# Searching the 256th largest indexer score: bit by bit, or by halving a guessed interval

## The chip, the core and the metric

The kernel runs on one core of a Trainium2 chip. The metric is the device time of one execution in microseconds, from the core's first instruction to its last. The engines named below are PE (TensorE), DVE (VectorE), ACT (ScalarE), POOL (GpSimd) and SP (SyncE, which here only issues transfers). Each engine takes its instructions in order, and an instruction that waits for another engine holds up all that stand behind it in its own queue.

## The reference, cut to what matters

A decoder block on 1024 tokens of width 1024: an indexed sparse attention and a latent attention side by side, merged by sigmoid gates, then a gated MLP. The part that the change touches is the choice of 256 keys for each query:

```python
iscore = jnp.einsum('bqh,bqhs->bqs', wib, jax.nn.relu(dots))
iscore = jnp.where(causal, iscore, -jnp.inf)
_, idx = lax.top_k(iscore, topk)          # topk = 256
ksel = k[bidx, idx]
...
sc = jnp.where(valid[:, :, None, None, :], sc, -jnp.inf)
p = jax.nn.softmax(sc, axis=-1)
```

Ties go to the lower column. The gates are `jax.nn.sigmoid(g_a)` and `jax.nn.sigmoid(g_b)`, with `g_a` and `g_b` two products of the normalised input with 1024 columns of `w_in` each.

## The kernel before, in words

Tokens are cut into 8 blocks of 128 queries. A program tests first whether the positions rise; if so the causal path runs, in which block b sees 128(b+1) keys, else a general path (`emit`, branch at L1808; the end of both is one drain at L1867). Blocks 0 and 1 have no more than 256 keys; for blocks 2 to 7 the kernel must find, in each of the 128 rows, the 256th largest of 384 to 1024 float32 scores.

`topk` does that for blocks 2, 3, 4 in one call and 5, 6, 7 in another. It takes the score as a 32-bit integer that is ordered as the score is: sixteen rounds settle its upper half, sixteen its lower half. A round counts in each block how many are below a candidate, on DVE by one instruction with an accumulator (L779), and for blocks 2 and 7 on ACT as a sum of signs (L776). Three small instructions on DVE then make the next candidate for three blocks at once (L787, L788, L789, 128x3 each). L760, L761, L802 and L804 make the integer halves. A tail of seven instructions for each block (L826 to L833) counts again in float32, ranks the ties with a scan (L829), and makes an additive mask of 0 or a large number, which SP writes to DRAM (L837) for the attention that comes later.

Three other streams of work are interleaved with the search.

- **Indexer.** PE makes the scores head by head (L702), ACT takes them from PSUM (L721), DVE adds them up (L726).
- **Gates.** 16 weight tiles of `w_g`, each a [128, 1024] piece in float32, used as a high and a low part. ACT makes the high part (L148), POOL the low part (L154). A tile gives two halves of 512 columns. A half is 24 products on PE (L178, L179, L180) into one of four PSUM banks; DVE takes it out and multiplies it with the norm's factor (L875); ACT applies the sigmoid (L877) and issues the write to DRAM (L878). In this text the halves are called #0 to #31. Eight small products (L557) stand ahead of #16.
- **Latents.** After #19 PE does 24 transposes (L896) in two groups of 12, into the same four PSUM banks. ACT and DVE take them out (L904, L905). Their inputs are eight loads by SP (L894) into six buffers: those of blocks 6 and 7 go where blocks 0 and 1 were. #20 to #27 follow, then the preparation of the latent attention.

The order on each engine is settled when the program is built, by priorities and due times of a scheduler; it is not written out in the source. The four banks mean that PE can finish a half only three halves (3 x 5.44 us) ahead of the one that DVE takes out. The high part of tile t stands in ACT's queue behind the sigmoid of half #(2t-4), so PE's first product of tile t (half #2t) also comes behind DVE's L875 of that half.

Of the kernel before, what the change touches and what calls it, by code (L numbers as in the profile page):

```python
# [50 lines left out]
LEAD = 1.0, 1.0  # L51
QDUP = 1
# [33 lines left out]
def chunks(W):  # L86
    """Column pieces of a row of W scores: (start, length), each in a PSUM bank of its own."""
    if W <= 512:
        return [(0, W)]
    return [(0, W // 2), (W // 2, W // 2)]  # L90


def weave(*lists, lead=1.0):
    """Call the closures of several lists, each list in its order, evenly mixed (the first list ahead, if lead < 1)."""
    items = [((k + 0.5) / len(x) * (1.0 if n else lead), n, f) for n, x in enumerate(lists) for k, f in enumerate(x)]
    for _, _, f in sorted(items, key=lambda t: t[:2]):
        f()


def skewed(first, second, lag):  # L100
    """The closures of two lists in turn, the second list some places behind."""
    out = []
    for k in range(len(first) + lag):
        out += first[k:k + 1] + (second[k - lag:k - lag + 1] if k >= lag else [])
    return out


class Block:
    def __init__(self, tc, a, out, causal, consts):
# [46 lines left out]
    def rsqrt(self, pool, y, x, n):  # L156
        """y = x ** -0.5 for [P, n] float32 tiles, x > 0."""
# [7 lines left out]
        for _ in range(3):  # L165
            # y = y * (1.5 - 0.5 * x * y * y)
# [8 lines left out]
    def mm3(self, ps, lhs, rhs, start, stop, **kw):  # L175
        """ps += lhs.T @ rhs, with both given as (hi, lo)."""
# [12 lines left out]
    def rope(self, x, c, s2, tmp):  # L189
        """x [P, H, 2, n] in place; c [P, H, n], s2 [P, H, 2, n] = (-sin, sin)."""  # L190
# [13 lines left out]
    def posmask(self, pool, b):  # L204
        """[P, S] bf16: 0 where pos[k] <= pos[q], BIG elsewhere, q in block b."""
# [10 lines left out]
    def view(self, off, shape, of=None):  # L216
        """A part of a region of float32r (r0, if no other), as an array of its own."""
# [16 lines left out]
    def run(self):  # L234
# [41 lines left out]
        if self.causal:  # L276
# [3 lines left out]
            self.topk(ta, [2, 3, 4], (2,))  # L280
# [17 lines left out]
        if self.causal:  # L298
            self.topk(tk, [5, 6, 7], (7,))
# [3 lines left out]
        # r1: v of the latent attention, the output of the indexed attention, half of w_out, then the operands of the  # L303
        # MLP's weights
# [17 lines left out]
        # the first scores; the last gates leave as they are, and take their sigmoid where they are used  # L322
# [35 lines left out]
        # tx: the other half of w_out, then three sums of the normalised rows  # L358
# [34 lines left out]
    def prologue(self):  # L393
# [18 lines left out]
        # cos and sin of pos * INV, [P, NB, 16]  # L412
# [32 lines left out]
        if self.causal:  # L445
            # 0 on and below the diagonal, BIG (tri) or FILL (trif) above it
# [8 lines left out]
            v.tensor_scalar(self.trif, jp, 0.0, FILL, op0=OP.is_gt, op1=OP.mult)  # L455
        self.posi = posi
# [17 lines left out]
    def stage(self, src):  # L474
        """A [P, n <= 1024] float32 array on its way from DRAM."""
# [4 lines left out]
    def ahead(self, name, *js):  # L480
        """Start the loads of weight pieces that wload will take later."""
# [20 lines left out]
    def wload(self, pool, name, j, wb, eng_hi="act", eng_lo="pool", tags=("wh", "wl")):  # L502
        """A [P, n <= 1024] piece of a weight as (hi, lo)."""
# [48 lines left out]
    def row_scales(self, halves):  # L552
        """R: the norm's factor of every token, on all partitions."""
# [11 lines left out]
    def cproj(self, w, ncols, blocks, pss=None):  # L565
        """Projections of token blocks; the row tiles in the outer loop, as they arrive."""
# [10 lines left out]
    def chunk_kv(self, rawx, w):  # L577
# [9 lines left out]
        # the raw projections; the norm's factor r goes into the factors of the three segments  # L587
# [23 lines left out]
        rt = self.t(c, [P, NB, 2, 16])  # L611
# [15 lines left out]
    def qstack(self, raw, scale, off):  # L627
        """[P, 8 * 2 * HD], every head twice -> [P, 8 * P] float32r, per head (hi; lo) of its transpose."""
# [9 lines left out]
    def twice(self, pool, x, nh, tag, bufs=2):  # L638
        """[P, nh * HD] -> [P, nh * 2 * HD], every head twice."""
# [12 lines left out]
    def chunk_iq(self, rp):  # L652
        """The indexer's queries and scores; the projections of the indexed attention's queries between."""
# [6 lines left out]
        def query(b, ps):  # L660
            # normalised, rotated
# [29 lines left out]
    def scores(self, lhs, rhs, W, diag=False):  # L691
        """psum [P, 2, 512] (or one bank used) of sum lhs[i].T @ rhs[i] over W columns; returns its view."""
# [15 lines left out]
    def indexer(self, q, b, marks):  # L708
        """Closures: the scores of a block of queries, head after head."""
# [28 lines left out]

    def topk(self, tk, blocks, on_act=()):
        """mask_d[b] = 0 for the TOPK largest of isc[b] (ties: the lower column first), BIG elsewhere.  # L740

        The TOPK-th largest value, bit by bit: first the upper halves of the values (as ordered 16 bit
        integers), then the lower halves among the values that share the upper half found. The columns of
        the blocks in on_act are counted by ACT, as a sum of signs; a candidate lies half way between two integers."""
# [26 lines left out]
        def below(src):  # L771
            """cnt: how many of src lie below c (or, by ACT, that less how many lie above)."""
# [9 lines left out]
        def search(src, first):  # L782
            """c: the largest integer that not more than thr lie below, of 16 bits from first on."""
# [8 lines left out]
        # keys: the lower half, in the order of the values, where the upper half is that found; 0 elsewhere  # L792
# [13 lines left out]
        # the whole value  # L806
# [10 lines left out]
        for j, b in enumerate(blocks):  # L817
# [7 lines left out]
            # le = score <= t; TOPK - #(score > t) = TOPK - W + #le  # L825
# [13 lines left out]
    def chunk_a(self, rp, name):  # L839
        """Closures: q (w_c3) or k and v (w_c4) of the indexed attention, normalised and rotated, to DRAM."""  # L840
# [44 lines left out]
    def latents(self, bx):  # L885
# [11 lines left out]
                # the shared rope part of k, four times over the partitions  # L897
# [41 lines left out]
            # v: [tok, head, hi | lo], odd heads lo | hi  # L939
# [38 lines left out]
    def project(self, pr):  # L978
        """Closures: the nope parts of q and k of the heads 2 * pr and 2 * pr + 1, into [P, 512] tiles."""
# [21 lines left out]
    def operands(self, st, pr, par):  # L1001
        """Closures: fill hq and hk of one parity out of the projected tiles."""
# [18 lines left out]
    def probs(self, pool, ps, W, mask, l, tag, bufs, wide=S):  # L1021
        """Softmax rows out of ps, the negated scaled scores; mask (bf16) adds BIG where a key is out."""
# [848 lines left out]
```

## Time and profile before

| | us |
|---|---|
| median of 3 runs (1672.86 to 1680.73) | 1673.42 |
| the profiled execution: its time is its span | 1673.4 |
| PE busy, whole span | 1533.1 (92%) |
| DVE busy, whole span | 1282.6 (77%) |
| POOL busy | 909.0 (54%) |
| ACT busy | 840.6 (50%) |
| DVE busy, 260 to 358 us | 97.19 of 98.00 |
| PE busy, 260 to 358 us | 76.11 of 98.00 |
| `topk`'s counts on DVE (L779) | 122.9, in 132 instructions |

The shares of the whole span say that PE bounds the kernel. The windows say that it does not do so everywhere: there is a stretch of some 150 us in which another engine is at 96 to 99% and PE is not. A table by stretch is therefore read before any table of the whole.

### The profile page before, as it was taken

The numbers are of one execution on the slowest core, as the hardware profiler recorded it, in microseconds if no ns is written. First come the engines' busy times: TensorE is split into PE (matmuls) and PEld (weight loads), VectorE is DVE, ScalarE is ACT, GpSimd is POOL, SyncE is SP. The second block draws the span as 40 slices with busy tenths as digits, with TensorE's granted clock in tenths as the row PEclk, the third lists the DMA queues.
The fourth block names the chain that finished last, engine by engine and source line by source line (L and its number), as shares of the span: only waits on it lengthen the run. The fifth ranks groups of instructions, "written<-read, shape, count | busy, mean of one in ns | idle before, by whom it ended". The sixth has DMA issues, their size and how long they took to land. (4 is left out here: it accounts for less than half of the span.)

```text
span 1673.4 us, 21977 instructions
## 1 busy us (share of the span) xinstructions
PE 1533.1 (92%) x7310; PEld 1254.1 (75%) x7310; DVE 1282.6 (77%) x2221; ACT 840.6 (50%) x1569; POOL 909.0 (54%) x748
## 2 busy tenths in 40 slices
PE   8889998758989999999999978999999999979995
PEld 7768886547767777898878776888888887858874
DVE  7368999998567887888461887677777775896996
ACT  3545645452437778877431454444444444434444
POOL 3241121221166677765560469877777773486683
PEclk9989998888999998999999989999999999999997
DMA  7331121231120003221664113222222213964333
GB/s 231 116 104 45 48 81 67 78 117 69 55 66 13 17 25 88 90 69 51 192 206 163 57 39 100 76 76 89 91 86 76 76 51 109 348 204 139 120 113 134
DMA packets 74844, 166.25 MB, mean 99 GB/s; under 512 B 9634, under 2 KB 14114, under 8 KB 74722
## 3 DMA queue, kind: packets, MB, share of 16 engines
q1 hardware_dynamic: 64496, 142.74, 26.4%
q10 hardware_dynamic: 7634, 13.64, 2.1%
q0 software_dynamic: 2592, 8.39, 1.3%
q8 instruction: 59, 0.97, 0.3%
q14 instruction: 63, 0.52, 0.1%
HBM read 123.94 MB, written 40.53 MB: 98 GB/s over the span
## 5 line engine op out<-in xcount | busy, mean ns | idle before, releaser
L178 PE MATMUL tc<-tc,tc 128*128 128x512 f32 (+2 forms) x1420 | 548.3, 390 | 25.1 <-ACT tc L148 14.6
L180 PE MATMUL tc<-tc,tc 128*128 128x512 f32 (+2 forms) x1420 | 549.5, 388 | 14.3 <-POOL tc L154 12.6
L179 PE MATMUL tc<-tc,tc 128*128 128x512 f32 (+2 forms) x1420 | 549.7, 387 | 0.5 <-POOL tc L154 0.4
L154 POOL TENSOR_TENSOR tc<-tc,tc 128x512 fp32r<-128x512 f32 (+2 forms) x182 | 293.4, 1619 | 295.4 <-ACT tc L148 271.5
L148 ACT ACTIVATE tc<-tc 128x512 fp32r<-128x512 f32 (+1 forms) x362 | 229.1, 658 | 339.2 <-PE tc L179 222.7
L178 PEld LDWEIGHTS tc<-tc,tc 128*128 128x128 f32 x1420 | 271.9, 192 | 85.2 <-ACT tc L148 16.6
L180 PEld LDWEIGHTS tc<-tc,tc 128*128 128x128 f32 x1420 | 271.0, 191 | 74.3 <-POOL tc L154 15.9
L179 PEld LDWEIGHTS tc<-tc,tc 128*128 128x128 f32 x1420 | 271.4, 191 | 55.7 <-POOL tc L154 0.9
L154 DVE TENSOR_TENSOR tc<-tc,tc 128x512 fp32r<-128x512 f32 x184 | 216.9, 1212 | 50.8 <-ACT tc L148 44.3
L179 PE MATMUL tc<-tc 128*128 128x512 f32 x332 | 132.6, 400 | 8.7 <-DVE tc L154 8.7
L1042 POOL TENSOR_SCALAR tc<-tc,tc 128x128 f32<-128x128 f32 (+7 forms) x128 | 95.2, 748 | 68.7 <-DVE tc L1041 56.1
L180 PE MATMUL tc<-tc 128*128 128x512 f32 x332 | 132.0, 399 | 0.4 <-DVE tc L154 0.4
L178 PE MATMUL tc<-tc 128*128 128x512 f32 x332 | 125.8, 401 | 7.1 <-ACT tc L148 7.0
L779 DVE TENSOR_SCALAR_CACHE_REDUCE tc<-tc,tc 128x512 bf16<-128x512 int16 (+7 forms) x132 | 122.9, 940 | 0.6
L1040 ACT ACTIVATE tc<-tc,tc 128x128 f32<-128x128 f32 (+7 forms) x128 | 96.3, 753 | 34.0 <-DVE tc L1034 14.5
L1574 DVE SCALAR_TENSOR_TENSOR tc<-tc,tc,tc 128x1023 f32<-128x1023 f32 x44 | 64.3, 1464 | 53.7 <-ACT tc L1573 53.6
L702 PE MATMUL tc<-tc 128*128 128x384 f32 (+4 forms) x352 | 92.1, 376 | 13.1 <-DVE tc L635 6.6
L776 ACT ACTIVATE tc<-tc,tc 128x384 bf16<-128x384 uint16 (+2 forms) x66 | 57.9, 877 | 79.1 <-DVE tc L789 57.2
L1575 DVE SCALAR_TENSOR_TENSOR tc<-tc,tc,tc 128x1022 f32<-128x1022 f32 x44 | 94.3, 2143 | 1.4
L702 PE MATMUL tc<-tc,tc 128*128 128x512 f32 (+4 forms) x288 | 78.8, 390 | 8.6 <-ACT tc L1040 8.2
L179 PEld LDWEIGHTS tc<-tc 128*128 128x128 f32 x332 | 63.7, 192 | 24.6 <-DVE tc L154 11.8
L178 PEld LDWEIGHTS tc<-tc 128*128 128x128 f32 x332 | 63.9, 193 | 22.1 <-ACT tc L148 8.5
(257 smaller groups left out, 2579.4 us busy)
## 6 DMA issues: line engine op xcount, KB each, us to landing
tc<-tc SPq DMA_DIRECT2D x144, 256.0 KB, 3.6
tc<-in_w_up SPq DMA_DIRECT2D x44, 512.0 KB, 4.0
tc<-in_w_down SPq DMA_DIRECT2D x77, 256.0 KB, 4.1
tc<-tc ACTq DMA_DIRECT2D x52, 256.0 KB, 2.0
tc<-tc SPq DMA_DIRECT2D x20, 512.0 KB, 2.6
tc<-in_w_g SPq DMA_DIRECT2D x16, 512.0 KB, 3.7
tc<-tc POOLq DMA_DIRECT2D x24, 256.0 KB, 2.6
tc<-in_w_c SPq DMA_DIRECT2D x10, 512.0 KB, 4.2
```

The costliest lines, as they stand in the source:

```text
L148: self.last_split = nc.scalar.activation(hi, src, AF.Copy)
L154: e.tensor_tensor(lo, src, hi.bitcast(F32), op=OP.subtract)
L178: x = [mm(ps, lhs[0], rhs[0], start=start, stop=False, **kw), mm(ps, lhs[0], rhs[1], start=False, stop=False, **kw), mm(ps, lhs[1], rhs[0] ...
L179: mm(ps, lhs[0], rhs[1], start=False, stop=False, **kw),
L180: mm(ps, lhs[1], rhs[0], start=False, stop=stop, **kw)]
L702: self.last_score = mm(ps[:, j * 512:j * 512 + n], l, r[:, o:o + n], start=i == 0, stop=i == len(lhs) - 1)
L776: nc.scalar.activation(junk2[:, :W], src[b], AF.Sign, bias=c[:, j:j + 1], scale=-1.0, accum_out=cnt[:, j:j + 1])
L779: v.tensor_scalar(junk[:, :W], src[b], c[:, j:j + 1], 0.0, op0=OP.is_lt, op1=OP.add, accum_out=cnt[:, j:j + 1])
L1040: self.last_exp = nc.scalar.activation(p3, src, AF.Exp, bias=nm, scale=-1.0, accum_out=l)
L1042: nc.gpsimd.tensor_scalar(p, p, l, 0.0, op0=OP.mult, op1=OP.add)
L1574: v.scalar_tensor_tensor(o[:, 1:], x[:, :S - 1], cw[:, t, 1:2], o[:, 1:], op0=OP.mult, op1=OP.add)
L1575: v.scalar_tensor_tensor(o[:, 2:], x[:, :S - 2], cw[:, t, 0:1], o[:, 2:], op0=OP.mult, op1=OP.add)
```

## The change

In `run`, both calls of `topk` on the causal path become calls of a new function `guess`, and a call of `unsure` follows the second. `guess` takes mean and standard deviation of a part of each row's scores (`bn_stats`, L768), guesses from them an interval that holds the 256th largest score, and halves it ten times. Each round is one float32 count for each block on DVE (L786) and three small instructions (L792 to L794); ACT counts nothing. A last count at the bound follows; the scores at or above the bound are pushed down (L800), the eight largest of what is left are taken (L801), and the one that the count points to is the threshold. The tail with ties, scan and mask (L815 to L824) is as before, with one small instruction more (L820) that notes rows where the result can't be the 256th. `unsure` adds these notes up on PE (L836) and sets a flag. `emit` reads the flag after the causal path (L1913), and runs the general path, with `topk` as before, where it is set. All other lines of the diff take comments out, or put one small buffer into another place, and set nine constants on POOL.

```diff
-            self.topk(ta, [2, 3, 4], (2,))
+            self.guess(ta, [2, 3, 4])
...
-            self.topk(tk, [5, 6, 7], (7,))
+            self.guess(tk, [5, 6, 7])
+            self.unsure()
...
+HALVINGS = 10
+SPAN = {2: (-1.5, 2.2), 3: (-0.3, 1.2), 4: (0.1, 1.1), 5: (0.3, 1.1), 6: (0.4, 1.1), 7: (0.5, 1.1)}
...
+    def guess(self, tk, blocks):
...
+        for j, b in enumerate(blocks):
+            m = b * P
+            k = 1 if m <= 512 else 2
+            for i in range(k):
+                v.bn_stats(stat[j][:, i], self.isc[b][:, i * m // k:(i + 1) * m // k])
+            v.bn_aggr(mv[:, j], stat[j][:, :k])
...
+        def above(j, b):
+            W = self.width(b)
+            x = self.t(tk, [P, wide], BF16, tag="junk", bufs=1)[:, :W]
+            v.tensor_scalar(x, self.isc[b], c[:, j:j + 1], 0.0, op0=OP.is_ge, op1=OP.add, accum_out=cnt[:, j:j + 1])
+            return x
+
+        for k in range(HALVINGS):
+            for j, b in enumerate(blocks):
+                above(j, b)
+            v.scalar_tensor_tensor(cp, h, -(2.0 ** -(k + 1)), c, op0=OP.mult, op1=OP.add)
+            v.scalar_tensor_tensor(m, cnt, TOPK - 0.5, h, op0=OP.is_ge, op1=OP.mult)
+            v.scalar_tensor_tensor(c, m, 2.0 ** -k, cp, op0=OP.mult, op1=OP.add)
+        v.scalar_tensor_tensor(c, h, 1.01 * 2.0 ** -HALVINGS, c, op0=OP.mult, op1=OP.add)
...
+        for j, b in enumerate(blocks):
+            x = above(j, b)
+            rest = self.t(tk, [P, wide], F32, tag="rest", bufs=1)[:, :self.width(b)]
+            v.scalar_tensor_tensor(rest, x, -3.0e38, self.isc[b], op0=OP.mult, op1=OP.add)
+            v.max(out=best[:, j], in_=rest)
+        v.tensor_scalar(m, cnt, -1.0, float(TOPK), op0=OP.mult, op1=OP.add)
...
+            v.tensor_scalar(bad[:, js], ct[:, W - 1:W], need[:, js], None, op0=OP.is_lt)
...
+        v.scalar_tensor_tensor(bad, need, 0.5, bad, op0=OP.is_lt, op1=OP.add)
...
-    with tc.If(rising > 0) as cmp:
-        Block(tc, a, out, True, {}).run()
-    with cmp.Else():
-        Block(tc, a, out, False, {}).run()
+    with tc.If(rising > 0):
+        Block(tc, a, out, True, {"redo": redo}).run()
+    again = nc.values_load(redo[0:1, 0:1], min_val=0, max_val=1)
+    with tc.If(again > 0):
+        Block(tc, a, out, False, {}).run()
```

In the program after the change lines have other numbers: L148 becomes L150, L477 L486, L726 L735, L837 L825, L875 L975, L877 L977, L878 L978, L894 L994, L896 L996, L905 L1005.

ACT's queue between the sigmoids of two successive halves in the gates, before:

```order
L877 ACTIVATE tc_1971<-tc_1971 128x512
L776 ACTIVATE tc_3158,tc_3153<-tc_3141,tc_3154 128x1024
L776 ACTIVATE tc_2364,tc_2359<-tc_2340,tc_2360 128x384
L878 DMA tc_103<-tc_1971 128x512
L776 ACTIVATE tc_3158,tc_3153<-tc_3141,tc_3154 128x1024
L776 ACTIVATE tc_2364,tc_2359<-tc_2340,tc_2360 128x384
L148 ACTIVATE tc_125<-tc_2091 128x1024
L877 ACTIVATE tc_2000<-tc_2000 128x512
```

and after:

```order
L977 ACTIVATE tc_1986<-tc_1986 128x512
L978 DMA tc_108<-tc_1986 128x512
L150 ACTIVATE tc_130<-tc_2106 128x1024
L977 ACTIVATE tc_2015<-tc_2015 128x512
L978 DMA tc_108<-tc_2015 128x512
```

The four counts ahead of the weight tile's high part are gone; each waited for a candidate that DVE made.

DVE's queue ahead of a gate half that it takes out, before (the end of a stretch of 19 instructions between two L875; `tc_3154` and `tc_2360` are the candidates of the two searches, which run side by side):

```order
L789 SCALAR_TENSOR_TENSOR tc_3154<-tc_3156,tc_3155 128x3
L789 SCALAR_TENSOR_TENSOR tc_2360<-tc_2362,tc_2361 128x3
L779 TENSOR_SCALAR tc_3157,tc_3153<-tc_3133,tc_3154 128x768
L787 TENSOR_SCALAR tc_3155<-tc_3154 128x3
L779 TENSOR_SCALAR tc_2363,tc_2359<-tc_2344,tc_2360 128x512
L787 TENSOR_SCALAR tc_2361<-tc_2360 128x3
L779 TENSOR_SCALAR tc_3157,tc_3153<-tc_3137,tc_3154 128x896
L779 TENSOR_SCALAR tc_2363,tc_2359<-tc_2348,tc_2360 128x640
L875 TENSOR_TENSOR tc_1971<-tc_1972,tc_1830 128x512
```

and after, between two halves of the second search:

```order
L975 TENSOR_TENSOR tc_2110<-tc_2111,tc_1845 128x512
L793 SCALAR_TENSOR_TENSOR tc_3066<-tc_3067,tc_3068 128x3
L794 SCALAR_TENSOR_TENSOR tc_3064<-tc_3066,tc_3065 128x3
L786 TENSOR_SCALAR tc_3132,tc_3067<-tc_1065,tc_3064 128x768
L792 SCALAR_TENSOR_TENSOR tc_3065<-tc_3068,tc_3064 128x3
L786 TENSOR_SCALAR tc_3134,tc_3067<-tc_1136,tc_3064 128x896
L786 TENSOR_SCALAR tc_3136,tc_3067<-tc_1207,tc_3064 128x1024
L975 TENSOR_TENSOR tc_2139<-tc_2140,tc_1846 128x512
```

One round of one search stands now between two halves, where two rounds of two searches stood.

SP's queue at the latents' last two loads, before:

```order
L477 DMA tc_3057<-in_w_g 128x1024
L477 DMA tc_3121<-in_w_g 128x1024
L894 DMA tc_2823<-tc_108 128x416
L894 DMA tc_2829<-tc_108 128x416
L837 DMA tc_106<-tc_3391 128x768
L837 DMA tc_106<-tc_3403 128x896
L477 DMA tc_3127<-in_w_g 128x1024
L837 DMA tc_106<-tc_3415 128x1024
```

and after:

```order
L825 DMA tc_111<-tc_3215 128x896
L486 DMA tc_2906<-in_w_g 128x1024
L486 DMA tc_2970<-in_w_g 128x1024
L486 DMA tc_3034<-in_w_g 128x1024
L825 DMA tc_111<-tc_3228 128x1024
L994 DMA tc_2736<-tc_113 128x416
L994 DMA tc_2742<-tc_113 128x416
L486 DMA tc_3040<-in_w_g 128x1024
```

The two loads stood ahead of the masks of blocks 5, 6 and 7; they now stand behind all three.

## Rows read from the trace of the kernel before

**Rows 1.** Windows (us): busy of PE, PEld, DVE, ACT, POOL; granted clock, DMA share, GB/s.

```profile
175.00:185.00 10.00, 6.09 (x30) 5.34 (x29) 9.97 (x21) 6.58 (x10) 2.36 (x1) 0.83 0.41 129
260.00:358.00 98.00, 76.11 (x298) 59.06 (x297) 97.19 (x252) 46.13 (x83) 23.42 (x11) 0.90 0.23 77
358.00:387.80 29.80, 8.34 (x30) 6.33 (x30) 28.68 (x71) 16.10 (x26) 3.38 (x4) 0.58 0.35 102
...
409.60:431.40 21.80, 21.80 (x99) 18.10 (x98) 2.81 (x5) 4.64 (x7) 4.78 (x2) 1.00 0.20 73
```

**Rows 2.** What PE waited for, 255 to 405 us: total, times, longest.

```profile
PE tc L896 <- DVE tc L875: 19.9, 3, 8.3
PE tc L178 <- ACT tc L148: 14.1, 4, 5.5
PE tc L180 <- POOL tc L154: 6.2, 5, 1.7
```

**Rows 3.** ACT's timeline around one weight tile: start, duration.

```profile
262.76 1.15 ACT L776 ACTIVATE tc<-tc,tc 128x1024 bf16<-128x1024 int16 x1 [2.03 <-DVE tc L789]
...
264.51 1.04 ACT L148 ACTIVATE tc<-tc 128x1024 fp32r<-128x1024 f32 x1
```

**Rows 4.** PE's timeline: last product of #7, first of #8, first of #20.

```profile
259.67 0.39 PE L180 MATMUL tc<-tc,tc 128*128 128x512 f32 x1
265.60 0.80 PE L178 MATMUL tc<-tc,tc 128*128 128x512 f32 x1 [5.54 <-ACT tc L148]
...
385.37 0.78 PE L178 MATMUL tc<-tc,tc 128*128 128x512 f32 x1
```

**Rows 5.** DVE's groups by line, 122 to 410 us: busy, mean ns, idle before.

```profile
L779 DVE TENSOR_SCALAR_CACHE_REDUCE tc<-tc,tc 128x512 bf16<-128x512 int16 (+7 forms) x132 | 122.9, 940 | 0.6
...
L789 DVE SCALAR_TENSOR_TENSOR tc<-tc,tc 128x3 f32<-128x3 f32 x64 | 11.5, 188 | 0.7
L779 DVE DVE_READ_ACCUMULATOR tc<-tc,tc 128x1 f32 x132 | 10.8, 82 | 0.0
...
L826 DVE TENSOR_SCALAR_CACHE_REDUCE tc<-tc,tc 128x384 bf16<-128x384 f32 (+5 forms) x6 | 5.6, 940 | 0.1
...
L833 DVE TENSOR_SCALAR tc<-tc 128x384 bf16<-128x384 bf16 (+5 forms) x6 | 2.0, 328 | 0.0
```

**Rows 6.** DVE's groups by line and shape, whole span.

```profile
L779 DVE TENSOR_SCALAR_CACHE_REDUCE tc<-tc,tc 128x896 bf16<-128x896 int16 x17 | 19.3, 1138 | 0.0
...
L726 DVE SCALAR_TENSOR_TENSOR tc<-tc,tc,tc 128x768 f32<-128x768 f32 x7 | 7.1, 1011 | 0.0
...
L1032 DVE TENSOR_REDUCE tc<-tc 128x1 f32<-128x768 f32 x8 | 7.6, 947 | 1.4 <-PE tc L702 1.4
...
L829 DVE TENSOR_TENSOR_SCAN tc<-tc 128x768 uint16<-128x768 bf16 x1 | 1.7, 1749 | 0.0
...
L826 DVE TENSOR_SCALAR_CACHE_REDUCE tc<-tc,tc 128x896 bf16<-128x896 f32 x1 | 1.1, 1145 | 0.0
```

**Rows 7.** DVE's timeline: two instructions during which POOL made a low part.

```profile
176.82 3.32 DVE L726 SCALAR_TENSOR_TENSOR tc<-tc,tc,tc 128x896 f32<-128x896 f32 x1
...
356.36 2.10 DVE L788 TENSOR_TENSOR tc<-tc,tc 128x3 f32<-128x3 f32 x1
```

**Rows 8.** Instructions of L875 (222 to 410 us), L896: count, ns min/median/max, first and last start.

```profile
L875 DVE TENSOR_TENSOR tc<-tc,tc x24: 675/683/692, 229.2 to 409.6; 128x512 f32<-128x512 f32 x24
...
L896 PE MATMUL tc<-tc,tc x24: 270/421/476, 357.8 to 385.3; 128*128 128x128 f32 x24
```

**Rows 9.** DMA issues, 372 to 376 us: the latents' last two loads, us to landing.

```profile
tc<-tc SPq DMA_DIRECT2D x2, 208.0 KB, 2.4
```

**Rows 10.** SP's instructions of the branch (L1808) and the register work (L1807).

```profile
L1808 SPq COMPARE_BRANCH  x2: 43/46/49, 5.1 to 1668.2; - x2
...
L1807 SPq TENSOR_LOAD <-fl x1: 464/464/464, 4.6 to 4.6; - x1
...
L1807 SPq FUSED_REGOPS  x1: 191/191/191, 1671.4 to 1671.4; - x1
```

More of the change, by code (lines that the diff above doesn't have):

```diff
@@ L455, in prologue @@
             v.tensor_scalar(self.trif, jp, 0.0, FILL, op0=OP.is_gt, op1=OP.mult)
+            self.count8 = self.t(c, [P, 8])
+            for k in range(8):
+                nc.gpsimd.memset(self.count8[:, k:k + 1], k + 1.0)
+            self.bad = self.t(c, [P, NB])
+            nc.gpsimd.memset(self.bad, 0.0)
         self.posi = posi
@@ L610, in chunk_kv @@
         v.tensor_tensor(x, x, self.gik[:, None, :].to_broadcast([P, NB, HD]), op=OP.mult)
-        rt = self.t(c, [P, NB, 2, 16])
+        rt = self.kd[:, 768:].rearrange("p (b t n) -> p b t n", b=NB, t=2)
         self.rope(braw[:, :, 0:16].rearrange("p b (t n) -> p b t n", t=2), self.cos[:, :, ::2],
@@ L737, in indexer, with small @@
         return [lambda h=h: one(h) for h in range(NH)] + [out]
+    def guess(self, tk, blocks):
+        nc = self.nc
+        v = nc.vector
+        n = len(blocks)
+        wide = self.width(blocks[-1])
+        def small(w=None):
+            return self.t(tk, [P, n] if w is None else [P, n, w], F32)
+        stat, mv = [self.t(tk, [P, 2, 6], F32) for _ in blocks], small(2)
+        for j, b in enumerate(blocks):
[4 more added lines that the diff above has]
+            v.bn_aggr(mv[:, j], stat[j][:, :k])
+        var = small()
+        v.tensor_copy(var, mv[:, :, 1])
+        i, y, sd, c, cp, m, cnt, h = self.t(tk, [P, n], I32), *[small() for _ in range(7)]
+        v.tensor_scalar(i, var.bitcast(I32), 1, None, op0=OP.logical_shift_right)
+        v.tensor_scalar(y.bitcast(I32), i, -1.0, 1597463007.0, op0=OP.mult, op1=OP.add)
+        v.tensor_mul(sd, var, y)
+        for j, b in enumerate(blocks):
+            js = slice(j, j + 1)
+            z, w = SPAN[b]
+            v.scalar_tensor_tensor(c[:, js], sd[:, js], z, mv[:, j, 0:1], op0=OP.mult, op1=OP.add)
+            v.tensor_scalar(h[:, js], sd[:, js], w, None, op0=OP.mult)
+        def above(j, b):
[10 more added lines that the diff above has]
+        v.scalar_tensor_tensor(c, h, 1.01 * 2.0 ** -HALVINGS, c, op0=OP.mult, op1=OP.add)
+        best, pick, thr, need = small(8), small(8), small(), small()
+        for j, b in enumerate(blocks):
+            x = above(j, b)
[3 more added lines that the diff above has]
+        v.tensor_scalar(m, cnt, -1.0, float(TOPK), op0=OP.mult, op1=OP.add)
+        v.tensor_tensor(pick, self.count8[:, None, :].to_broadcast([P, n, 8]), m[:, :, None].to_broadcast([P, n, 8]),
+                        op=OP.is_equal)
+        v.tensor_tensor(pick, pick, best, op=OP.mult)
+        v.tensor_reduce(thr, pick, axis=AX.X, op=OP.add)
+        bad = self.bad[:, blocks[0]:blocks[0] + n]
+        for j, b in enumerate(blocks):
+            W = self.width(b)
+            t0, js = thr[:, j:j + 1], slice(j, j + 1)
+            ne = self.t(tk, [P, wide], BF16, tag="junk", bufs=1)[:, :W]
+            eq = self.t(tk, [P, wide], BF16, tag="eq", bufs=1)[:, :W]
+            ct = self.t(tk, [P, wide], U16, tag="ct", bufs=1)[:, :W]
+            v.tensor_scalar(ne, self.isc[b], t0, 0.0, op0=OP.is_le, op1=OP.add, accum_out=cnt[:, js])
+            v.tensor_scalar(need[:, js], cnt[:, js], float(TOPK - W), None, op0=OP.add)
+            v.tensor_scalar(eq, self.isc[b], t0, None, op0=OP.is_equal)
+            v.tensor_tensor_scan(ct, eq, eq, 0.0, op0=OP.add, op1=OP.bypass)
+            v.tensor_scalar(bad[:, js], ct[:, W - 1:W], need[:, js], None, op0=OP.is_lt)
+            v.scalar_tensor_tensor(eq, ct, need[:, js], eq, op0=OP.is_le, op1=OP.mult)
+            v.tensor_sub(ne, ne, eq)
+            mb = self.t(tk, [P, wide], BF16, tag="mb", bufs=1)[:, :W]
+            v.tensor_scalar(mb, ne, BIG, None, op0=OP.mult)
+            nc.sync.dma_start(self.mask_d[b, :, :W], mb)
+        v.scalar_tensor_tensor(bad, need, 0.5, bad, op0=OP.is_lt, op1=OP.add)
@@ L739, in topk, with unsure @@
+    def unsure(self):
+        nc = self.nc
+        total = self.t(self.cst, [P, 1])
+        nc.vector.tensor_reduce(total, self.bad, axis=AX.X, op=OP.add)
+        ones = self.t(self.cst, [P, 1])
+        nc.gpsimd.memset(ones, 1.0)
+        ps = self.psA()
+        nc.tensor.matmul(ps[:1, :1], total, ones, start=True, stop=True)
+        nc.vector.tensor_scalar(self.redo, ps[:1, :1], 0.5, None, op0=OP.is_gt)
     def topk(self, tk, blocks, on_act=()):
@@ L1777, with emit @@
 IDX_SC = HD ** -0.5
-def emit(tc, a, out):
+def emit(tc, a, out, keep):
     nc = tc.nc
+    redo = keep.tile([1, 1], I32, name="redo")
     with tc.tile_pool(name="flag", bufs=1) as p, tc.tile_pool(name="flagp", bufs=1, space=PSUM) as pp:
@@ L1797, in emit @@
         v.memset(ones, 1.0)
+        v.memset(redo, 1)
         nc.scalar.activation(mn, ones, AF.Copy)
@@ L1867 @@
     with tile.TileContext(nc, schedule_with_timeline_sim=True) as tc:
-        emit(tc, a, out)
+        with tc.tile_pool(name="keep", bufs=1) as keep:
+            emit(tc, a, out, keep)
     r = _run(nc, [{f"in_{k}": v for k, v in arrays.items()}], core_ids=[0])
```

## The prediction

> **What bounds the kernel now.** I read the busy times by stretch first, since the whole span hides the place. From 260 to 358 us DVE is busy 97.19 of 98.00 us, PE 76.11, and PE's granted clock is 0.90; from 358 to 387.8 DVE has 28.68 of 29.80, PE 8.34, the clock is 0.58 (2.4 GHz for part of it, 1.2 for the rest). From 409.6 on PE is busy without a gap at clock 1.00 [rows 1]: there four halves of 24 products take 21.8 us, so a half costs PE 5.44 us. DVE takes out 24 halves between 229.2 and 409.6 us [rows 8], one per 7.84 us. So halves #0 to #19 and the latents go at DVE's pace, not PE's.
>
> Next, what ended PE's waits: the latents' transposes wait 19.9 us for L875, the first products of a weight tile 14.1 us for ACT's split, 6.2 us for POOL's [rows 2]. ACT's split is late since it stands behind counts that wait for DVE's next candidate: L776 idles 2.03 us for L789, and L148 comes after it [rows 3]. POOL's part is late because ACT's is. All three rows lead back to DVE. An example: PE ends #7 at 260.06 and starts #8 at 265.60, 5.54 us later [rows 4].
>
> From 385.37, where #20 begins [rows 4], PE no longer waits, though DVE still works on the last masks until 409. **The start of #20 is therefore the point to forecast**: what comes after it on PE is the same work, and moves with it.
>
> **What goes.** DVE loses the integer counts, 122.9 us and 10.8 us of accumulator reads [rows 5], with their small instructions; ACT loses L776. On ACT nothing waits for it then but the sigmoid of the half before, so its removal is worth nothing of its own beyond the waits above. What DVE gets instead decides.
>
> **Where DVE starts.** #7 ends at 260.06 and PE had run #0 to #7 without a gap, so #0 ended 7 x 5.44 us earlier, at 222.0. DVE took it out only at 229.2 [rows 8], 7.2 us late. In the new order 29 narrow counts stand ahead of that, where 68 stood, so DVE will be there in time, and wait. Further ahead, 175 to 185 us has PE busy for 6.09 of 10.00 us at clock 0.83 [rows 1], while one L726 of 896 columns takes 3.32 us beside POOL's low part [rows 7], where 768 columns take 1.011 on average [rows 6]. Part of that idling is the counts' doing, part the hold, which stays: between 0 and 5 us to gain, I take 3. So #0 ends at 219 (217 to 222).
>
> **DVE's work from there to the last mask**, by the new order, in which all of it stands ahead of the L975 of #18:
> - 19 halves taken out, 0.683 us each [rows 8]: 13.0.
> - 37 counts, 33 of them eleven rounds of blocks 5, 6 and 7. Their middle width, 896 in float32, took 1.145 us before (the tail's L826 [rows 6]) and 0.082 for the read [rows 5]: 33 x 1.227 = 40.5, and 4 narrow ones of some 0.9: 44.1 together.
> - 46 small instructions at L789's 0.188 [rows 5]: 8.7.
> - L800, like L726 with 1.011 at 768 columns [rows 6], six blocks of 704 columns on average: 5.6. L801, the eight largest, is in no row. If it is one pass it is like the reduction L1032, 0.947 at 768; if it is slow it is like the scan L829, 1.749 [rows 6]. That gives 5.2 or 9.6; I take 5.2, since it too reads one input once and writes next to nothing.
> - The tail, six lines from L826 to L833, 33.3 us in all in the view by line [rows 5], and L820: 34.
> That is 110.6. To this come holds. L788, as small as L789 with its 0.188 [rows 5], took 2.10 beside POOL [rows 7]. POOL makes nine low parts in this stretch, 2.36 us each. If each caught a small instruction at its beginning it would be 20 us; but a new round has 3.7 us of counts to each group of small instructions, so that a part is met somewhere in its course or not at all. I take 7, and 0 and 20 as ends. The sum is **118 us, to 337**.
>
> PE by itself would end #19 at 219 + 19 x 5.44 + 2.1 (the eight products ahead of #16) = 324.5 (those eight at 0.27, the shortest transpose [rows 8]). DVE falls behind by about 7 us up to #8 and more at the tails, 12 to 17 us at most. Four banks let PE run 16.3 us ahead, so I expect single waits of a few us in #12 to #18, and the latents to wait for DVE.
>
> **The latents.** #18 and #19 are taken out right after the last mask. PE then transposes blocks 0 and 1 (six at 0.42, the median, clock down [rows 8]): 340. Only then are two buffers free for blocks 6 and 7, whose loads now stand behind the last mask on SP; that mask is issued at 337, so it is not the later of the two. They land 2.4 us after issue [rows 9]: 342.5. Six transposes more: **#20 starts at 345** instead of 385.4, a gain of 40.4. The loads of weight tiles stand behind masks too (tiles 10 and 11 behind that of block 5, due at some 315 us); they have 25 us until they are needed, which covers the landing and both splits. Without that cover a tile late by its landing and two splits (some 7 us) would cost that once.
>
> `unsure` puts one product into PE's queue in the preparation after the gates. It waits for DVE's flag sum, ready at 337; PE comes there some 45 us later (eight halves at 5.44). Nothing. The constants on POOL and the moved small buffer lie ahead of the indexer beside other work: nothing.
>
> **The end of the program.** Before, SP's last jump starts at 1668.2 and the next instruction at 1671.4, 3.2 us [rows 10]. That far jump remains, now over the second block, whose condition is false. New are the load of the flag (0.46 as at the start [rows 10]), a compare and register work (0.05 and 0.19), and two jumps over nothing or little, each between nothing and 3.2 us. Between 0.7 and 7.1; I take 2.5, nearer to the low end as both targets lie next to the jump. The Trainium skill ("Runtime: NRT & Kernel Launch", section "Instruction fetch mechanics") says that a taken branch stalls for a fetch where its target is outside the two pages at hand; by it the short jumps would be free and the cost 0.7. No row here shows a short jump that is taken.
>
> **Sum**: 1673.4 (span, which equals the median of the runs) - 40.4 + 2.5 = 1635.5, say **1635**.
>
> **Rivals.**
> - *DVE stays the bound for longer.* Holds of 20 (+13), L801 at the scan's price (+4.4), #0 at 222 (+3), and 7 at the end (+4.6): 1660. For it speaks that the trace shows L801 nowhere, and that every hold row is near 2 us; against it that no row is bad at the same time as the others. Above 1658: 0.08.
> - *The float32 counts cost more than the integer ones.* If 16-bit inputs had a faster rate, the 44.1 us would be bound by a price that the old counts don't have. The rows say no: at 896 columns int16 took 1138 ns with the accumulator, float32 1145 [rows 6]. A price higher by three quarters would add 33 us, #20 at 378, 1668. Chance 0.02. The Trainium skill ("VectorE: DVE Perf Modes", section "The perf-mode tier table (the rule you actually need)") has this rule: bf16 at 4x, 693 ns, float32 at 2x, 1227 ns, for 2048 elements, a ratio of 1.77. The trace disagrees for the accumulating form.
> - *Slower: the general path runs as well.* The flag is set as soon as one of 768 rows has over eight scores between the bound and the 256th (or its interval misses). Then a whole second pass follows, of the same products and with masks at full width: at least another 1630 us, so over 3,260. It decides at one row. Against it: worked through with draws of the reference's inputs, the 256th lies one to eight places below the bound in every row. For it: eight is the edge, it is reached in block 6, and rounding on the chip may differ. 0.04.
> - *Better.* No holds, DVE never limits PE: #19 ends at 324.5 or two earlier, then the 24 transposes at 0.27 (6.5) and the load's landing: #20 at 331 to 334, 1621 to 1625. With a gain by the new order of the attention's instructions of some us more, below 1618: 0.05.
>
> **How the numbers follow.** The forecast and its bounds, 1618 to 1658, have the rest, 0.81. This is the range: its low end is PE's own pace with some us for the order, its high end the dearest prices but one. Half a per cent, about what a measurement can tell, is 8.4 us: 1665 to 1682 is the same. Faster: 0.81 + 0.05 + 0.06 of the first rival = 0.92; same 0.04 (the rest of that one, and the second); slower 0.04.
>
> **What would show it.** In the trace after: #20 begins near 345 us; DVE's L975 of #0 follows PE's end of #0 within 1 us, and it idles ahead of it; no ACT instruction between sigmoid and split; L786 at 1.15 for 896 columns, L801 at 1.1; small instructions of 1 to 2 us only beside POOL's low parts; the wait of L996 for L975 is under 15 us (19.9 before), PE's for ACT's split under 5; the last L824 near 337; the end of the program 2 to 3 us longer behind the last write. If #20 is at 345 and the time is not 40 lower, something later took the gain back; if #20 is late with L786 and L801 as priced, the holds were mis-sized.

## The result, and the profile after

The changed kernel takes 1616.33 us (median of 4, 1614.80 to 1622.71) where the kernel before takes 1674.26: a ratio of 0.966, 95% interval 0.964 to 0.968. It gets faster, as forecast, but by 58 us instead of 38, and ends 1.7 us below the range of 1618 to 1658. The profiled execution has a span of 1615.5.

Windows of the changed kernel, columns as in [rows 1]; the stretches from 260 us on are cut at the latents (324) and at 350:

```profile
175.00:185.00 10.00, 7.85 (x50) 7.02 (x49) 9.87 (x17) 5.32 (x7) 1.37 (x1) 1.00 0.32 111
222.00:260.00 38.00, 38.00 (x169) 31.47 (x169) 38.00 (x87) 8.04 (x10) 8.39 (x4) 1.00 0.28 90
260.00:324.00 64.00, 63.41 (x285) 52.32 (x283) 62.98 (x107) 16.52 (x22) 27.81 (x11) 1.00 0.38 125
324.00:350.00 26.00, 21.44 (x88) 17.68 (x89) 9.92 (x17) 8.01 (x12) 2.99 (x3) 0.80 0.25 88
350.00:371.80 21.80, 21.80 (x98) 18.05 (x97) 2.77 (x4) 4.43 (x6) 4.79 (x2) 1.00 0.22 73
```

From 260 to 324 us PE is busy 63.41 of 64.00 at clock 1.00, where it had 76.11 of 98.00 at 0.90 [rows 1]. DVE is nearly as busy as before, 62.98 of 64.00, and yet holds nobody up. From the start of PE's last product of a half to the L975 that takes this half out pass 0.5 to 13.3 us in #0 to #19, always less than the 16.3 us that four banks let PE run ahead; before, it was 7.4 to 27.0. The two longest of PE's waits from 255 to 405 us, and where #20 begins:

```profile
PE tc L996 <- DVE tc L975: 3.9, 2, 2.6
PE tc L996 <- DMA tc<-tc: 1.3, 2, 0.7
```

```profile
334.08 0.78 PE L180 MATMUL tc<-tc,tc 128*128 128x512 f32 x1
```

The waits for ACT's and POOL's splits [rows 2] are gone. DVE takes out #0 at 219.1 and #27 at 379.1:

```profile
L975 DVE TENSOR_TENSOR tc<-tc,tc x28: 656/685/692, 219.1 to 379.1; 128x512 f32<-128x512 f32 x28
```

Half #20 begins at 334.08, not at 385.37 [rows 4] and not at the 345 of the forecast.

**Where the 57.9 us of the profiled executions came from**, by the same instruction in both traces: 51.3 by the start of #20; 52.2 by the L975 of #27 (431.3 and 379.1; the clock is down for a shorter time); 54.8 at the first instruction of the MLP's convolution, and 61.2 at its last; 59.4 at PE's last product; 57.9 at the end. So 6.4 us were gained in the up projection, far behind the change, on work that the change doesn't touch. The other differences behind #27 (2.6 us gained up to the convolution, 1.8 lost behind it) have no cause that these runs show. The lines are those of the convolution on DVE, one for every piece of the up projection: count, ns, first and last start; before, then after.

```profile
L1574 DVE SCALAR_TENSOR_TENSOR tc<-tc,tc,tc x44: 1279/1284/2319, 1004.8 to 1426.5; 128x1023 f32<-128x1023 f32 x44
```

```profile
L1674 DVE SCALAR_TENSOR_TENSOR tc<-tc,tc,tc x44: 1279/1284/2330, 950.0 to 1365.3; 128x1023 f32<-128x1023 f32 x44
```

421.7 us and 415.3. One step of it in a window, before and then after (same products, columns as above):

```profile
1124.45:1166.68 42.23, 42.23 (x182) 34.01 (x181) 32.63 (x25) 20.66 (x29) 33.91 (x20) 1.00 0.21 76
```

```profile
1068.88:1110.31 41.43, 41.43 (x182) 34.02 (x181) 33.09 (x25) 20.71 (x29) 33.91 (x20) 1.00 0.22 77
```

PE is busy without a gap at clock 1.00 in both, and takes 0.80 us less for the same 182 entries. Averaged over the up projection, from the start of one product of 512 columns to the start of the next, it is 233.3 ns before and 228.9 after.

DVE in the changed kernel: groups of the new search from 100 to 400 us (columns as in [rows 5]), and its timeline around one round (start, duration):

```profile
L786 DVE TENSOR_SCALAR_CACHE_REDUCE tc<-tc,tc 128x512 bf16<-128x512 f32 (+5 forms) x66 | 61.7, 939 | 0.5
...
L793 DVE SCALAR_TENSOR_TENSOR tc<-tc,tc 128x3 f32<-128x3 f32 x20 | 7.1, 357 | 0.1
...
L801 DVE MAX8 tc<-tc 128x8 f32<-128x384 f32 (+5 forms) x6 | 5.3, 889 | 0.0
...
L794 DVE SCALAR_TENSOR_TENSOR tc<-tc,tc 128x3 f32<-128x3 f32 x20 | 4.0, 198 | 0.2
```

```profile
276.39 0.08 DVE L786 DVE_READ_ACCUMULATOR tc<-tc,tc 128x1 f32 x1
276.39 0.69 DVE L975 TENSOR_TENSOR tc<-tc,tc 128x512 f32<-128x512 f32 x1
276.99 0.15 DVE L793 SCALAR_TENSOR_TENSOR tc<-tc,tc 128x3 f32<-128x3 f32 x1
...
278.43 1.15 DVE L786 TENSOR_SCALAR_CACHE_REDUCE tc<-tc,tc 128x896 bf16<-128x896 f32 x1
279.50 0.08 DVE L786 DVE_READ_ACCUMULATOR tc<-tc,tc 128x1 f32 x1
...
280.94 1.62 DVE L793 SCALAR_TENSOR_TENSOR tc<-tc,tc 128x3 f32<-128x3 f32 x1
```

The second fence shows two things. Successive records overlap: L975 lasts 0.69 us, but the next instruction starts 0.60 after it; the read of the accumulator starts before the count's record ends, together with what follows. And L793, two inputs in SBUF, takes 1.62 us where its median is 0.154; POOL's low part runs from 280.15 to 282.54:

```profile
280.15 2.39 POOL L156 TENSOR_TENSOR tc<-tc,tc 128x1024 fp32r<-128x1024 f32 x1 [7.46 <-ACT tc L150]
```

The end of the program on SP:

```profile
L1911 SPq COMPARE_BRANCH  x2: 38/41/44, 5.1 to 1608.8; - x2
```

```profile
L1910 SPq FUSED_REGOPS  x1: 186/186/186, 1609.0 to 1609.0; - x1
```

```profile
L1913 SPq TENSOR_LOAD <-redo x1: 797/797/797, 1609.3 to 1609.3; - x1
```

```profile
L1914 SPq EVENT_SEMAPHORE  x8: 17/17/17, 1612.7 to 1613.2; - x8
L1914 SPq COMPARE_BRANCH  x1: 50/50/50, 1610.2 to 1610.2; - x1
```

The new short jump costs 0.2 us (1608.8 to 1609.0), the load 0.80, the far jump over the general block 2.5 (1610.2 to 1612.7) where it was 3.2 [rows 10]: 1.5 us in all.

### The profile page after: what moved, and what is told of

Its sections match the earlier page's. It is cut to its first block, busy times and chain, and to the rows that moved or that the text cites. A ratio compares the mean times of both kernels' runs of the same rounds, so it can differ in the third digit from the quotient of the medians.

```text
span 1615.5 us, 21528 instructions
## 1 busy us (share of the span) xinstructions
PE 1514.8 (94%) x7312; PEld 1248.7 (77%) x7312; DVE 1210.2 (75%) x1959; ACT 783.0 (48%) x1437; POOL 918.4 (57%) x758
## 5 line engine op out<-in xcount | busy, mean ns | idle before, releaser
L156 POOL TENSOR_TENSOR tc<-tc,tc 128x512 fp32r<-128x512 f32 (+2 forms) x182 | 300.8, 1659 | 246.0 <-ACT tc L150 229.4
L150 ACT ACTIVATE tc<-tc 128x512 fp32r<-128x512 f32 (+1 forms) x362 | 230.3, 659 | 350.0 <-PE tc L181 219.9
L156 DVE TENSOR_TENSOR tc<-tc,tc 128x512 fp32r<-128x512 f32 x184 | 223.1, 1245 | 45.4 <-ACT tc L150 38.8
L181 PEld LDWEIGHTS tc<-tc 128*128 128x128 f32 x332 | 63.9, 192 | 31.2 <-DVE tc L156 18.6
L180 PEld LDWEIGHTS tc<-tc 128*128 128x128 f32 x332 | 63.3, 192 | 18.9 <-ACT tc L150 5.4
L711 PEld LDWEIGHTS tc<-tc 128*128 128x128 f32 x352 | 61.5, 194 | 18.0 <-DVE tc L644 6.5
L182 PEld LDWEIGHTS tc<-tc 128*128 128x128 f32 x332 | 64.0, 193 | 14.6 <-DVE tc L156 1.5
```

The source lines that it names most:

```text
L150: self.last_split = nc.scalar.activation(hi, src, AF.Copy)
L156: e.tensor_tensor(lo, src, hi.bitcast(F32), op=OP.subtract)
L180: x = [mm(ps, lhs[0], rhs[0], start=start, stop=False, **kw), mm(ps, lhs[0], rhs[1], start=False, stop=False, **kw), mm(ps, lhs[1], rhs[0] ...
L181: mm(ps, lhs[0], rhs[1], start=False, stop=False, **kw),
L182: mm(ps, lhs[1], rhs[0], start=False, stop=stop, **kw)]
L711: self.last_score = mm(ps[:, j * 512:j * 512 + n], l, r[:, o:o + n], start=i == 0, stop=i == len(lhs) - 1)
```

## The experiments

Two questions stood open. What shortened the up projection? And what sets the pace of the gates' stretch, before and after: DVE's work, ACT's queue, or PE itself?

**Addresses.** The tiles of the constants are allocated ahead of the others, so their sizes shift what lies behind. The change replaces a tile of 1 KB there and adds three small ones. In the built programs I took, for each of the 4932 products of 512 columns, the distance between the start addresses of its two operands in SBUF (the operand of 512 columns less the weights), modulo 256 bytes. Before: 2160 products at 0, 2052 at 224, 384 at 32, 336 at 192. After: 2160 at 0, 2052 at 64, 720 at 192. The up projection has 224 before, 64 after.

e1, the kernel before with 32 bytes more (e2 adds the same two lines behind `self.bad` in the changed kernel, e6 with 16 elements instead of 8):

```diff
             v.tensor_scalar(self.trif, jp, 0.0, FILL, op0=OP.is_gt, op1=OP.mult)
+            self.pad = self.t(c, [P, 8])
+            nc.gpsimd.memset(self.pad, 0.0)
```

> The kernel before, with one unused tile of 32 bytes per partition among the constants, so that nearly every buffer behind it starts 32 bytes later; all instructions but one memset are the same. In the kernel before, 2436 of the 4932 products of 512 columns have operands whose start addresses differ by 32 modulo 64; here 336. Theory (PE takes about 233 ns from product to product where they differ, 227 to 229 where they agree): the up projection of the MLP (1000 to 1390 us) gets 6 to 7 us shorter, the time 1665 to 1669. Rival (what the changed kernel gained after 1000 us came from the order of its instructions or from run to run): 1674, the up projection as long as before.

> The changed kernel with the same unused tile of 32 bytes. The changed kernel has no product whose operands differ by 32 modulo 64; here 2772 do. Theory of the addresses: 1622 to 1627, with 233 ns from product to product in the up projection. Rival: 1616, 229 ns.

Measured: e1 1672.35 against 1674.15, ratio 0.999 (0.997 to 1.000), no change; e2 1622.58, ratio 0.969 (0.966 to 0.972). The same line of the convolution in e1 and e2:

```profile
L1576 DVE SCALAR_TENSOR_TENSOR tc<-tc,tc,tc x44: 1279/1284/2318, 999.3 to 1421.7; 128x1023 f32<-128x1023 f32 x44
```

```profile
L1676 DVE SCALAR_TENSOR_TENSOR tc<-tc,tc,tc x44: 1277/1287/2318, 947.8 to 1370.8; 128x1023 f32<-128x1023 f32 x44
```

422.4 and 423.0 us. e2 agrees with the theory: 32 bytes take the whole gain of the up projection back. e1 does not, it missed the 1665 to 1669 of the theory: agreement modulo 64 was not enough. In e1 the up projection has the distance 192 modulo 256, the changed kernel 64. So I formed the rule anew, modulo 256, from the four traces, and tried it where it makes a large difference. e5 is the kernel before with 224 bytes, so that the distance there is 0; one small buffer had to move, as in the changed kernel, to make room:

```diff
-        rt = self.t(c, [P, NB, 2, 16])
+        rt = self.kd[:, 768:].rearrange("p (b t n) -> p b t n", b=NB, t=2)
...
+            self.pad = self.t(c, [P, 56])
+            nc.gpsimd.memset(self.pad, 0.0)
```

> The kernel before, with one small buffer put where the changed kernel has it and an unused tile of 224 bytes, so that the buffers behind start elsewhere; the instructions are the same but for one memset. Read from the first runs: what counts is the distance of the two operands' start addresses modulo 256: at 0 a product takes 227 ns to the next, at 64 229, at 32, 96 (modulo 128) and 192 it takes 233. In the kernel before the up projection (1764 products of 512 columns) has 224; here 0, and 4596 of 4932 products in all have 0 instead of 2160. Theory: 6.4 ns on each of 1764 products and some 2 us elsewhere, 1660 to 1664. Rival (the residue was by chance, the change did something else to the up projection): 1672 to 1676, as with 32 bytes.

> The changed kernel with an unused tile of 64 bytes: all 4932 products have the distance 0 modulo 256, instead of 2160 with 0, 2052 with 64 and 720 with 192. Theory of the addresses: the up projection goes from 229 to 227 ns a product (3.7 us), and 720 others from 233 to 227 (up to 4.5 us where PE sets the pace): 1608 to 1613. Rival: 1616.

Measured: e5 1660.86 against 1672.94, ratio 0.9925 (0.9905 to 0.9945); e6 1607.91, ratio 0.961 (0.959 to 0.963). The line in e5, then in e6:

```profile
L1576 DVE SCALAR_TENSOR_TENSOR tc<-tc,tc,tc x44: 1281/1429/2426, 1003.2 to 1413.6; 128x1023 f32<-128x1023 f32 x44
```

```profile
L1676 DVE SCALAR_TENSOR_TENSOR tc<-tc,tc,tc x44: 1282/1285/2330, 945.4 to 1357.5; 128x1023 f32<-128x1023 f32 x44
```

410.4 and 412.1 us, from 421.7 and 415.3. Both fall where the rule puts them (1660 to 1664, 1608 to 1613, the second by 0.1 us below). A kernel gets 12 us faster, and another 8, by nothing but where its buffers lie.

**Who sets the pace.** e8 leaves all counts of the kernel before to DVE:

```diff
-            self.topk(ta, [2, 3, 4], (2,))
+            self.topk(ta, [2, 3, 4])
...
-            self.topk(tk, [5, 6, 7], (7,))
+            self.topk(tk, [5, 6, 7])
```

> The kernel before with ACT's counts on DVE as well: no count stands in ACT's queue, and DVE has 66 counts more (33 of 384 and 33 of 1024 columns, some 62 us). Theory (DVE's work set the pace, ACT's late splits followed from it): 1715 to 1735. Rival (the counts in ACT's queue made the weights late): faster than 1674, some 1650.

Measured: 1712.84, ratio 1.024 (1.021 to 1.027), slower by 40 us, 2 below the theory's range. The three longest of PE's waits from 215 to 440 us, then the lines that make the masks, before and in e8:

```profile
PE tc L896 <- DVE tc L875: 14.1, 2, 9.2
PE tc L178 <- ACT tc L148: 13.4, 5, 4.8
PE tc L180 <- POOL tc L154: 9.9, 7, 1.7
```

```profile
L833 DVE TENSOR_SCALAR tc<-tc x6: 253/327/426, 326.8 to 409.0; 128x384 bf16<-128x384 bf16 x1, 128x512 bf16<-128x512 bf16 x1, 128x640 bf16<-128x640 bf16 x1, 128x768 bf16<-128x768 bf16 x1
```

```profile
L833 DVE TENSOR_SCALAR tc<-tc x6: 248/345/2429, 395.5 to 476.6; 128x384 bf16<-128x384 bf16 x1, 128x512 bf16<-128x512 bf16 x1, 128x640 bf16<-128x640 bf16 x1, 128x768 bf16<-128x768 bf16 x1
```

No count is in ACT's queue any more, and PE waits for ACT's split nearly as it did (13.4 us, 14.1 in [rows 2]). The splits are late here since the sigmoid ahead of them waits for DVE: ACT's L877 waits 192.3 us for L875 from 215 to 480 us. The last mask is made 67.6 us later. On DVE it stood between #22 and #23 and stands behind #27 now, so more of PE's halves are done ahead of it: #28 is taken out 44.9 us later, and 40 show at the end.

e4 adds work to DVE in the changed kernel:

```diff
-HALVINGS = 10
+HALVINGS = 13
```

> The changed kernel with 13 halvings instead of 10 in both calls: three rounds more of 2.5 us (blocks 2 to 4) and of 3.75 us (blocks 5 to 7) on DVE, 18.7 us in all. Theory (DVE still sets the pace from 155 us to the last mask): number 20 begins 17 to 19 us later, 1632 to 1636. Rival (PE sets the pace now, DVE's work has room in the four banks): 1616 to 1622.

Measured: 1618.46, ratio 0.966 (0.964 to 0.969), 2 us above the changed kernel. My theory fell, the rival held: in the changed kernel PE sets the pace up to the latents. Its windows and waits:

```profile
260.00:324.00 64.00, 63.97 (x287) 52.79 (x285) 63.23 (x124) 16.29 (x22) 22.77 (x11) 1.00 0.34 117
324.00:350.00 26.00, 15.13 (x59) 11.82 (x60) 25.68 (x43) 6.43 (x10) 1.86 (x3) 0.74 0.25 87
```

```profile
PE tc L996 <- DVE tc L975: 5.3, 2, 4.0
PE tc L996 <- DVE tc L816: 4.7, 1, 4.7
```

PE loses nothing up to 324. The rounds come out behind, where the latents wait for DVE (last mask at 351.3 instead of 326.6), and #20's L975 is 7.6 us later. By 662 us, in the attention, the same product starts only 1.3 us later than in the changed kernel; in the up projection it is 2.9, at PE's last product 0.3. Which waits hide the rest stays open.

e9 and e10 do one of the two searches the new way:

```diff
-            self.guess(tk, [5, 6, 7])
+            self.topk(tk, [5, 6, 7], (7,))
```

> One part of the change alone: blocks 2 to 4 by the new search, 5 to 7 by the old one with ACT's counts of block 7. Distances of the operands as in the changed kernel (7 us of its gain). Theory (DVE sets the pace of the old kernel, PE that of the new; DVE's work was some 75 us too long, PE can use only some 50 of it): DVE loses about 36 us, number 20 begins some 30 us earlier, 1630 to 1642. Rival (the work is all that counts, half of it brings half): 26 us and the 7, 1641 to 1645. Second rival (ACT's counts ahead of the splits set the pace): those of block 7 stay, under 15 us gain, above 1658.

> The other part alone: 5 to 7 by the new search, 2 to 4 by the old one with ACT's counts of block 2. Same theories: 1630 to 1642 where PE is the limit that cuts the gain, 1641 to 1645 where half brings half, above 1658 where ACT's counts set the pace.

Measured: e9 1652.18, ratio 0.988 (0.986 to 0.990); e10 1641.63, ratio 0.982 (0.979 to 0.985). Against the kernel before, e9 brings 21 us, e10 31, with some 7 us of each due to addresses (the convolution takes 415.0 and 414.4 us, 421.7 before). All three theories missed e9; e10 lies on the edge between the first two. The masks tell why: the last one is made 26 us earlier in e9 and 51 in e10 (383.0 and 357.7, from 409.0). In e9 it is that of block 7; in e10, where the new search has made the masks of blocks 5 to 7 by 355.3, it is that of block 4. The old search's masks in e9, then in e10:

```profile
L933 DVE TENSOR_SCALAR tc<-tc x3: 345/369/427, 370.5 to 383.0; 128x768 bf16<-128x768 bf16 x1, 128x896 bf16<-128x896 bf16 x1, 128x1024 bf16<-128x1024 bf16 x1
```

```profile
L933 DVE TENSOR_SCALAR tc<-tc x3: 244/278/314, 339.7 to 357.7; 128x384 bf16<-128x384 bf16 x1, 128x512 bf16<-128x512 bf16 x1, 128x640 bf16<-128x640 bf16 x1
```

The halves of the search are not alike, as I had assumed. On DVE, each record counted no further than the start of the next, the search of blocks 2 to 4 took 76.5 us before and takes 47.6 in the changed kernel; that of blocks 5 to 7 took 124.1 and takes 79.4. So the second gives 45 us, the first 29. Most of the difference is in the instructions of three elements a row, 10.7 us in the first search before and 26.5 in the second: all nine that took over 0.8 us from 233 to 362 us, up to 2.3, belong to the second and stand beside a low part of POOL. In both runs PE still waits for DVE at the latents, 16.9 us in e9 and 10.9 in e10. Less the addresses the two gains are 14 and 24, 38 together; the whole brings 51. With one search left as it was, DVE still holds up the latents.

**The price of the guess missed.** e12 sets the flag always:

```diff
-        nc.vector.tensor_scalar(self.redo, ps[:1, :1], 0.5, None, op0=OP.is_gt)
+        nc.vector.tensor_scalar(self.redo, ps[:1, :1], -1.0, None, op0=OP.is_gt)
```

> The changed kernel with the flag set whatever the notes say (threshold -1 instead of 0.5): the general path runs behind the causal one. The price of one row that the guess misses: over 3260 as forecast, since the general path makes masks and scores at full width in all 8 blocks; my estimate 3600 to 4000.

Measured once: 4027.03, 27 above my estimate of 3600 to 4000.

```profile
span 4025.2 us, 46859 instructions
```

One row of 768 that the guess misses would cost 2,411 us, some 40 times what the guess brings.

**A faster kernel.** What PE still lost was at the latents. e3 puts them behind #27:

```diff
-        self.latents(lat)
-        lat_close()
-        self.b_weights(bx)
-        tk, tk_close = self.pool("tk", 1)
-        self.gates(wg, go, range(NEXT if self.causal else 0, MID))
+        if self.causal:
+            self.gates(wg, go, range(NEXT, MID))
+        self.latents(lat)
+        lat_close()
+        self.b_weights(bx)
+        tk, tk_close = self.pool("tk", 1)
+        if not self.causal:
+            self.gates(wg, go, range(0, MID))
```

> The changed kernel with the latents' transposes behind the gate halves 20 to 27 instead of ahead of them. If what is left of the wait there (11.0 us for work of 6.5, and the clock down behind it) is DVE's last tail, the halves cover it and the time is 3 to 6 us lower, 1610 to 1613. Rival: the next stage needs the latents at once, and waits for ACT and DVE to take them out: within 2 us of 1616, or slower.

> Both: the latents behind the gate halves, and the 64 bytes. If the two gains are independent, 1600 to 1605, lower than the kernel before and the changed one. If the latents' gain was in part one of addresses, 1606 to 1610.

> The kernel with late latents and 64 bytes, and 13 halvings instead of 10, 18.7 us more on DVE. Theory (PE sets the pace there, and DVE has until the latents, behind number 27): 1598 to 1602, as with 10. Rival (DVE still has no room, its extra rounds hold PE through the four banks): 1605 to 1618.

Measured: e3 1608.55, ratio 0.961 (0.959 to 0.964), 1.5 us below the range expected. e7, with the 64 bytes, 1599.39, ratio 0.9555 (0.9534 to 0.9577): the two gains add up, and this is the fastest kernel of the study, 73.6 us below the kernel before measured beside it. e11, with 13 halvings, 1602.45, ratio 0.959 (0.955 to 0.963): 0.45 us above the theory's range and 2.5 below the rival's. Its interval overlaps with that of e7, so three more halvings cost little or nothing there. The transposes in the changed kernel, then in e7:

```profile
L996 PE MATMUL tc<-tc,tc x24: 271/422/477, 323.1 to 334.0; 128*128 128x128 f32 x24
```

```profile
L1001 PE MATMUL tc<-tc,tc x24: 270/273/329, 367.1 to 371.8; 128*128 128x128 f32 x24
```

4.7 us from first to last, at a median of 273 ns, where the changed kernel needs 10.9 at 422: no wait for DVE, and the clock stays up (granted 1.00 from 324 to 370 us in e7, 0.80 from 324 to 350 in the changed kernel).

## Why the prediction was right or wrong, step by step

- **What bounds the kernel, and where**: right. DVE in the gates' stretch; in e8, with no count in ACT's queue, PE still waits 13.4 us for ACT's split, and the kernel is slower. That fits the forecast that taking the counts from ACT is worth nothing of its own; no run takes them away without giving DVE more or less work.
- **#0 at 219**: right, its L975 begins at 219.1. DVE idles ahead of it, as forecast, but for 0.46 us only. The trace before has 34 counts on DVE ahead of the first L875, not the 68 of the forecast.
- **DVE's work of 118 us from there to the last mask**: the mis-sized term, and the first step that failed. It took 107.8 from the L975 of #0 to that of #18, just behind the last mask (lines below). The durations were well priced: the records of this stretch sum up to 120.6. What failed is that I added durations. Records of successive instructions overlap, by 61 ns on average over 209 records here: 12.8 us. [rows 7] showed no neighbours, and I didn't look for them; the start of the next instruction is the price.

```profile
326.59 0.43 DVE L824 TENSOR_SCALAR tc<-tc 128x1024 bf16<-128x1024 bf16 x1
326.93 1.28 DVE L975 TENSOR_TENSOR tc<-tc,tc 128x512 f32<-128x512 f32 x2
```

- **Prices within it**: the float32 count 939 ns on average, as the integer count's 940 [rows 5]; so the rival of the dearer counts fell. The tier rule of the Trainium skill ("VectorE: DVE Perf Modes", "The perf-mode tier table (the rule you actually need)") would have had the 16-bit form faster; the trace shows no such gain for the form with accumulator. L801, in no row before, 5.3 us against 5.2: one pass. The holds were put at 7, with 20 as the end: L793 has 5.8 us in 11 instructions of this stretch where L794 has 1.7 in 11, and the other lines' excess brings it to some 13. So the holds were 6 too low and the other durations 3 too high. POOL made 14 low parts in this stretch, not nine.
- **PE by itself at 324.5, and single waits in #12 to #18**: PE came to the transposes at 323.1, and waited for no weight: with 10 us less on DVE the four banks were enough.
- **The latents**: 8 us from the last mask to #20 forecast, 7.1 measured (from the end of L824 at 327.0).
- **"What comes after it on PE is the same work, and moves with it"**: wrong, the second step that failed. The work was the same, its addresses were not. The up projection gave 6.4 us more; e2, e5 and e6 show that the distance of the operands does it. With the operands apart by 32 (e2), where the up projection goes as slowly as in the kernel before, the changed kernel takes 1622.58, inside the range.
- **The end of the program**: 1.5 us instead of 2.5, within its bounds; the short jump is close to free. The rule of the Trainium skill quoted there ("Runtime: NRT & Kernel Launch", "Instruction fetch mechanics") fits the trace: 0.2 us for the short jump that is taken, 2.5 for the far one.
- **The rivals**: the time of "better" came true (#20 at 331 to 334), for another reason: it supposed no holds. The time below 1618 had a chance of 0.05, for a gain by the order of the attention's instructions; the gain came by the addresses of the up projection. The slower rival's price, over 3,260, is 4,027 (e12); it did not occur with these inputs.

In numbers: forecast 40.4 - 2.5 = 37.9; 10.9 more up to #20 (10 of it by DVE, 0.9 by the latents), 8.1 from there to PE's last product (6.4 of it in the up projection), 1.0 at the end: 57.9. Either failed step alone would have left the time in the range: 1635.5 less 10.9 is 1624.6, less 8.1 it is 1627.4. Both together leave it.

## What to carry to other kernels

Where one engine feeds another through a few banks, price the feeder by the distance from start to start in the timeline, not by the durations of its records, and then check which of the two is the slower: here the change brought DVE below PE's pace, and what had been the bound took 19 us more work almost for nothing. A change of a small tile's size moves every buffer allocated behind it; before a gain or loss far from the edit is put down to the edit, compare the operands' addresses in the two programs. A fast path with a check is worth its gain only as often as the check holds; the price of a miss should be measured once.

## What the runs showed of the hardware that I had not expected

The time from one float32 product of 512 columns to the next, with PE busy throughout at full clock, goes by the distance of its two operands' start addresses in SBUF, modulo 256 bytes. In the up projection it is 226.7 ns at 0 (e6), 228.9 at 64 (the changed kernel), and 233.3 at 32 (e2), 192 (e1) and 224 (the kernel before). It is the distance, not where one operand lies: over the whole of nine programs (these five, e3, e5, e7 and e10), with the 512 columns at 224 modulo 256, weights at 224 give 227.4, at 160 229.2, and at 192, 32 and 0 233.3; and with both operands at the same place modulo 256 (0, 32, 160, 192 or 224) it is 227 to 228. Distances of 96 (e10) and 160 (e5) stood only in the first stage, at 233 to 234; 128 stood nowhere. With all products at 0 (e6) the first stage too went from 233.4 to 227.0, but from 137 to 200 us both kernels stand at the same product within 0.2 us; PE is not busy throughout ahead of that, 48.86 of 55.00 us from 100 to 155 in the changed kernel. Why the distance matters, these runs do not show.

The second is that DVE's records mostly overlap by 60 to 90 ns (median 77 in the stretch above), and that an instruction of three elements a row with two inputs in SBUF can take 1.6 us beside a low part of POOL, in another round 2.29, where its median is 0.154.
